# Latent attention scores in an fp32 encoder layer: six full matmuls per query tile, or four and a pair in row groups

## The chip, the cores and the metric

The kernel runs on one core of one Trainium2 chip. The core has a matrix engine (TensorE, PE in the profile), with its weight loads shown apart as PEld, and VectorE (DVE), ScalarE (ACT), GpSimd (POOL) and SyncE (SP). SP only issues transfers here. The metric is the time of one execution in device microseconds; before the change it is 1594.84 us, the median of two runs (1594.51 and 1595.16).

## The reference

One encoder layer is applied to two token sequences (256 and 1024 tokens, width 1024). A combined input projection feeds two attention groups: multi-head latent attention with 8 heads (MLA) and 2-D neighbourhood attention with 8 heads (NA). The outputs are normalised, projected, added to the input, and a SwiGLU feed-forward layer follows. The change touches the scores of the latent attention alone:

```python
q = (rmsnorm(c_q, q_norm_g) @ w_uq).reshape(B, S, MLA_HEADS, MLA_QK_DIM)
kv = (rmsnorm(c_kv, kv_norm_g) @ w_ukv).reshape(...)
k_nope, v = kv[..., :MLA_NOPE_DIM], kv[..., MLA_NOPE_DIM:]
q = concatenate([q[..., :64], apply_rope(q[..., 64:], cos, sin)], -1) * 96 ** -0.5
k_rope = apply_rope(k_r, cos, sin)           # one for all heads
s = einsum(qi[..., :64], k_nope) + einsum(qi[..., 64:], k_rope)
p = softmax(s)
o = einsum(p, v)
```

So a score sums over 96 features: 64 that each head has for itself ("nope") and 32 rotary ones, whose keys all heads share.

## The kernel before, in words

All large products are made from numbers split in two, a high part `h` and a rest `l`, both in the type fp32r. A product is then hh + hl + lh: three matmuls that accumulate in one PSUM bank (`mm3`, lines 109 to 113). The scores use it too: with 96 rows in use of the 128 (64 nope rows, 32 rotary rows, 32 rows set to zero by `zero_spare`), a query tile of 128 queries against 1024 keys takes two halves of 512 keys with three matmuls each, six in all.

The stages follow one another: latents and rotary parts, NA projections, NA itself, MLA (the stage of the change), output projection, feed-forward. MLA goes over four pairs of heads (`PAIRS`, index `p`). In a pair, `attend` handles blocks of 256 queries: `c` counts four such blocks of the long sequence ("sample"), `i` the two heads of the pair. So there are 4 x 4 x 2 = 32 sample blocks with two query tiles `u` each, and 8 blocks of the short sequence ("prompt"). For a query tile, TensorE makes the scores `S` (1024 keys, two PSUM banks; two such tiles exist, `S0` and `S1`), DVE takes the row maximum `mm`, ACT the exponential `ex` with its sum, TensorE transposes `ex` in eight pieces into `tp`, and ACT and DVE split them into `PT`. TensorE then multiplies `PT` with the values (`o`, 16 matmuls for a block) and transposes the result back twice (`os`, `ob`); POOL adds the halves, scales (`at`), and ACT's queue stores to `a_d`. Between blocks, the projections of the next pair's queries and keys run (`project_pair`, `project_rest`, tiles `SH`), which borrow the banks of `S0` for that time.

Queries lie in tiles `mq` (slots A, B, C in turn), keys in `mk` (slots e, o). Their rotary rows are read from DRAM (`rope_d`, `kr_d`), put there by an earlier stage; their nope rows are split out of PSUM by `put_q` and `split_k`.

A scheduler orders the instructions of every engine but one. SP's are left in the order of the program text (`manual_schedule` with SP), so a load that waits there for its tile to come free holds back all loads behind it. Transfers by `load_r` go on SP's queue, those by `store_r` on ACT's.

Of the kernel before, what the change touches and what calls it, by code (L numbers as in the profile page):

```python
# [19 lines left out]
P = 128  # L20
# [9 lines left out]
DH = 64  # L30
# [10 lines left out]
def encoder_trunk(ctx: ExitStack, tc: tile.TileContext, x_tm, x_T, g_attn, w_c, w_v, w_qk,  # L41
# [544 lines left out]
    def small_w(src, n):  # L586
        raw = lw.tile([P, 512], F32, name="w2_raw", bufs=2)
# [5 lines left out]

    cT = [[None] * 5 for _ in range(2)]
# [9 lines left out]
    def make_V():  # L604
# [9 lines left out]
        for i in range(2):  # L614
            for x in (q_slot[1][i], q_slot[2][i]):
                zero_spare(x, i)
# [6 lines left out]

    def q_tile(p, i, ch):
        x = qp_slot[i] if ch == 0 else q_slot[(2 * p + ch - 1) % 3][i]
        r0, hrow = 64 - 32 * i, 32 * ((2 * p + i) % 4)
        a, n = CHUNKS[ch]
        load_r(x[r0:r0 + 32],
               rope_d[p // 2, :, hrow:hrow + 32, a:a + n].rearrange("s p t -> p s t"))
        return x  # L630

    def k_tile(p, i, ch):
# [3 lines left out]
        if p < 2 and (ch == 1 or p == 0):  # L636
# [4 lines left out]
    def put_q(x, i, ps):  # L641
        rs = slice(64 * i, 64 * i + 64)
        split_ps_scaled(x[rs, 0], x[rs, 1], ps[rs], QSCALE)
# [13 lines left out]
    def split_k(K, ch, o, n, ps):  # L657
# [3 lines left out]
        for i in range(2):  # L661
            rs = slice(64 * i, 64 * i + 64)
            nc.vector.tensor_sub(out=K[i][ch][rs, 1, o:o + n], in0=ps[rs],
                                 in1=K[i][ch][rs, 0, o:o + n])

    def project_first():
# [3 lines left out]
        wq = small_w(w_qn[0], 3)  # L670
        K = [[k_tile(0, i, ch) for ch in range(2)] for i in range(2)]
        for s in range(2):
            load_cT(0, 3, s)
        for c in range(2):
            raw = lw.tile([P, 512], F32, name="w2_raw", bufs=2)
# [5 lines left out]
        for i in range(2):  # L681
            for x in (q_slot[0][i], qp_slot[i]):
                zero_spare(x, i)
# [3 lines left out]
        def body(bank):  # L687
# [13 lines left out]
            for i in range(2):  # L701
                put_q(Q[i][0], i, ps[:, 256:512])
# [10 lines left out]
    def project_pair(p):  # L713
# [5 lines left out]
        def body(bank):  # L719
# [7 lines left out]
            for i in range(2):  # L727
                put_q(Q[i][0], i, ps)
# [15 lines left out]
    def attend(p, Q, K, c_lo, c_hi, sample, between=None):  # L744
# [6 lines left out]
        for c in range(c_lo, c_hi):  # L751
            for i in range(2):
# [8 lines left out]
                else:  # L761
                    both = rp.tile([P, 2, 2, 256], F32R, name="PT", bufs=6)
                    pt = [[both[:, 0]], [both[:, 1]]]
                for u in range(2):
# [30 lines left out]
                for u in range(2):  # L795
# [6 lines left out]
                nc.gpsimd.tensor_tensor(out=ob[:, :, 0], in0=ob[:, :, 0], in1=ob[:, :, 1],  # L802
                                        op=ALU.add)
                if i == 0:
                    at = p2.tile([P, 2, P], F32, name="at", bufs=2)
                nc.gpsimd.tensor_tensor(out=at[:, :, i * DH:(i + 1) * DH], in0=ob[:, :, 0],
# [977 lines left out]
```

## Time and profile before

| | |
|---|---|
| median of the runs | 1594.84 us |
| the profiled execution's own time | 1593.86 us |
| its span | 1591.8 us |
| PE busy | 1559.4 us (98%), 8560 matmuls |
| PEld busy | 1394.9 us (88%) |
| DVE, ACT, POOL busy | 1016.4, 760.2, 766.4 us |
| MLA, about 380 to 672 us of the span: share of the span | 18% |

Busy time on PE is the union of its records. A record runs from the start of a matmul to its modelled end, so records of matmuls that follow one another overlap; how much time a matmul takes from TensorE is read from the distance of starts, not from its duration. The trace names a line of a helper where a helper issues the instruction: `L111`, `L112` and `L113` are the three matmuls of `mm3`, whoever calls it.

### The profile page before, as it was taken

The page shows a single profiled execution, that of the slowest core. Times are in us where ns is not written, and L with a number is a line of the kernel's source. Part 1 is how long each engine was busy: PE and PEld are TensorE (multiplying, and loading weights), DVE is VectorE, ACT ScalarE, POOL GpSimd, SP SyncE. Part 2 cuts the span into 40 slices and gives each one's busy share as a digit, 9 for nine tenths or more (in the row PEclk, how much of TensorE's full clock was granted, in tenths as well). Part 3 has the DMA queues.
Part 4 walks back from the last instruction along what each step waited for, and adds up shares of the span by engine and source line. Part 5 has one row for each costly group of instructions (what it writes and reads, how often), then busy time and mean ns, then how long its engine had stood idle before and what let it go on. Part 6 is the DMA issues. An engine that isn't in the chain of part 4 may idle for free.

```text
span 1591.8 us, 23991 instructions
## 1 busy us (share of the span) xinstructions
PE 1559.4 (98%) x8560; PEld 1394.9 (88%) x8560; DVE 1016.4 (64%) x1656; ACT 760.2 (48%) x1552; POOL 766.4 (48%) x961
## 2 busy tenths in 40 slices
PE   8999999999999999999999999999999999999998
PEld 8888789998888888877799999999999988888886
DVE  5754035556777777535698766566766666886676
ACT  6534144455777777633344344444334353443334
POOL 4632235544211119359626888788888871010002
PEclk9999999999999999999999999999999999999999
DMA  8626022243101021285573232223322237843434
GB/s 288 206 73 167 17 54 64 38 169 107 32 15 30 20 97 38 69 274 202 193 247 110 85 103 78 100 88 111 111 77 98 83 131 286 292 120 99 151 104 157
DMA packets 118022, 190.38 MB, mean 120 GB/s; under 512 B 34960, under 2 KB 65424, under 8 KB 115344
## 3 DMA queue, kind: packets, MB, share of 16 engines
q1 hardware_dynamic: 85216, 162.64, 31.4%
q10 hardware_dynamic: 31872, 23.14, 4.6%
q0 software_dynamic: 816, 3.08, 0.5%
q8 instruction: 67, 1.10, 0.3%
q14 instruction: 51, 0.42, 0.1%
HBM read 128.92 MB, written 59.90 MB: 119 GB/s over the span
## 4 chain that ended last, share of the span: by engine, by line
PE 83%; POOL 6%; DMA 3%; DVE 3%; ACT 3%; issue 2%; SPq 0%; POOLq 0%; ACTq 0%; DVEq 0%
PE M L113 10%; PE M L111 10%; PE M L112 10%; PE d L111 6%; PE d L113 6%; PE d L112 6%; PE o L789 4%; PE tp L779 3%; PE na_o L513 3%; PE pj L111 2%; PE pj L112 2%; PE pj L113 2%; PE S L111 2%; PE S L113 2%; PE S L112 2%
## 5 line engine op out<-in xcount | busy, mean ns | idle before, releaser
L1242 DVE TENSOR_TENSOR C<-M,C 128x428 f32<-128x428 f32 (+1 forms) x263 | 151.0, 594 | 144.0 <-issue 68.1
L1023 POOL TENSOR_TENSOR wr<-wt,wr 128x512 fp32r<-128x512 f32 (+1 forms) x106 | 148.9, 1405 | 67.4 <-ACT wr L1021 67.3
L1021 ACT CAST wr<-wt 128x512 fp32r<-128x512 f32 (+1 forms) x106 | 63.2, 599 | 134.2 <-PE M L112 123.7
L111 PE MATMUL M<-s,wr 128*128 128x428 f32 x352 | 125.9, 358 | 1.2 <-ACT x L970 1.2
L112 PE MATMUL M<-s,wr 128*128 128x428 f32 x352 | 125.4, 356 | 0.0
L113 PE MATMUL M<-s,wr 128*128 128x428 f32 x352 | 125.3, 357 | 0.0
L101 DVE TENSOR_TENSOR PT<-tp,PT 128x512 fp32r<-128x512 f32 (+1 forms) x144 | 93.4, 658 | 35.4 <-ACT PT L100 34.2
L1244 ACT COPY C<-M 128x428 f32<-128x428 f32 (+1 forms) x128 | 63.3, 514 | 84.6 <-PE M L113 84.6
L111 PE MATMUL M<-x,wr 128*128 128x428 f32 x264 | 94.2, 357 | 1.5 <-DVE C L1242 1.4
L100 ACT CAST PT<-tp 128x512 fp32r<-128x512 f32 (+1 forms) x144 | 79.4, 568 | 33.4 <-PE tp L779 30.2
L802 POOL TENSOR_TENSOR ob<-ob 128x128 f32<-128x128 f32 x40 | 18.4, 461 | 158.5 <-ACT ob L799 155.1
L771 DVE TENSOR_REDUCE mm<-S 128x1 f32<-128x1024 f32 (+1 forms) x80 | 85.0, 1062 | 13.8 <-PE S L113 12.3
L113 PE MATMUL M<-x,wr 128*128 128x428 f32 x264 | 91.5, 357 | 0.5 <-POOL wr L1023 0.3
L112 PE MATMUL d<-SE 128*128 128x512 f32 (+1 forms) x238 | 91.7, 387 | 0.0
L111 PE MATMUL d<-SE 128*128 128x512 f32 (+1 forms) x238 | 89.6, 388 | 0.0
L113 PE MATMUL d<-SE 128*128 128x512 f32 (+1 forms) x238 | 89.6, 387 | 0.0
L1284 ACT CAST SE<-as 128x640 fp32r<-128x640 f32 x58 | 42.2, 727 | 94.8 <-issue 57.2
L773 ACT ACTIVATE ex<-S,mm 128x1024 f32<-128x1024 f32 (+1 forms) x80 | 79.8, 998 | 14.9 <-DVE mm L771 13.6
L779 PE MATMUL tp<-ident,ex 128*128 128x128 f32 x544 | 79.2, 274 | 2.4 <-DVE PT L101 1.3
L789 PE MATMUL o<-PT,v 128*128 128x256 f32 x544 | 80.6, 287 | 0.8 <-ACT PT L100 0.8
L90 POOL TENSOR_SCALAR ry<-ssy 128x1 f32<-128x1 f32 x5 | 4.1, 820 | 157.6 <-ACT yo L1574 157.5
L111 PE MATMUL M<-SE,wr 128*128 128x428 f32 x220 | 78.6, 357 | 0.3 <-ACT C L1244 0.3
(466 smaller groups left out, 4909.1 us busy)
## 6 DMA issues: line engine op xcount, KB each, us to landing
as<-act_d SPq DMA_DIRECT2D x73, 320.0 KB
act_d<-C SPq DMA_DIRECT2D x70, 320.0 KB
w<-in_w_down_dram SPq DMA_DIRECT2D x44, 256.0 KB
x<-in_x_tm_dram SPq DMA_DIRECT2D x20, 512.0 KB
wr<-wop_d SPq DMA_DIRECT2D x20, 512.0 KB
wraw<-in_w_gate_dram SPq DMA_DIRECT2D x10, 1024.0 KB
wraw<-in_w_up_dram SPq DMA_DIRECT2D x10, 1024.0 KB
wop_d<-wr SPq DMA_DIRECT2D x18, 512.0 KB
```

The costliest lines, as they stand in the source:

```text
L100: i = nc.scalar.copy(out=hi, in_=ps)
L101: nc.vector.tensor_sub(out=lo, in0=ps, in1=hi)
L111: nc.tensor.matmul(out, lhsT=sh, rhs=mh, start=first, stop=False, **kw)
L112: nc.tensor.matmul(out, lhsT=sh, rhs=ml, start=False, stop=False, **kw)
L113: return nc.tensor.matmul(out, lhsT=sl, rhs=mh, start=False, stop=last, **kw).ins
L771: nc.vector.reduce_max(out=nm[:, u:u + 1], in_=S, axis=AX.X, negate=True)
L773: nc.scalar.activation(ex, S, AF.Exp, bias=nm[:, u:u + 1], scale=1.0, accum_out=l[:, u:u + 1])
L779: nc.tensor.transpose(tp[:, j], ex[:, kt * P:(kt + 1) * P], ident)
L789: nc.tensor.matmul(oT, lhsT=vv, rhs=pt[s][g][:, j], start=kt == 0 and s == 0, stop=kt == nkt - 1 and s == 1)
L1023: i1 = (eng or nc.gpsimd).tensor_tensor(out=lo, in0=raw_, in1=hi, op=SUB)
L1242: evicted[0] = nc.vector.tensor_add(out=o, in0=ps[:, 0:XN[j]], in1=o).ins
L1244: nc.scalar.copy(out=o, in_=ps[:, 0:XN[j]])
```

## The change

For the sample blocks the 288 rows of a score (three products of 96) are laid out anew. A query tile and a key tile have two planes of 128 rows each. For one head of a pair, with its own 64 rows first:

| rows | plane 0, query x key | plane 1, query x key |
|---|---|---|
| own 64 | q_h x k_h (nope) | q_l x k_h (nope) |
| other 64 | rotary: q_h x k_l and q_l x k_h, 32 rows each | q_h x k_l (nope) |

What is left is the rotary q_h x k_h, 32 rows. It is made by matmuls of 32 rows from two new tiles: `k_rot` holds the rotary keys' high part four times, in partitions 0, 32, 64, 96 (keys 0 to 511 and 512 to 1023, twice), and `rot` the rotary queries of one block, once for each of these. A query tile so takes four matmuls of 128 rows and two of 32 rows, which lie in two different row groups of the array (groups 0 and 1 for `u` = 0, groups 2 and 3 for `u` = 1). Prompt blocks keep `mm3`.

With it: `put_q` copies the high query part a second time, on ACT; `split_k` writes the rest of the keys into the other half and copies the high part once more, on POOL; the rows set to zero go for sample tiles; `rot_tile` issues four small loads per block, on SP, or on ACT's queue for `c` of 1 to 3 in the last pair; `w2_raw` has one buffer and no longer two; in the last pair's `c` of 2 and 3 the two operations on `ob` and `at` run on DVE and no longer on POOL.

```diff
+    k_rot = rslot["p2"].tile([P, 512], F32R, name="k_rot")
...
+    def halves_of(i):
+        return slice(64 * i, 64 * i + 64), slice(64 - 64 * i, 128 - 64 * i)
...
+    def rot_tile(p, i, c):
+        x = p2.tile([P, P], F32R, name="rot", bufs=3)
+        hrow, a = 32 * ((2 * p + i) % 4), NTOK_P + 256 * c
+        for u in range(2):
+            for g in range(2):
+                o = 64 * u + 32 * g
+                (store_r if p == PAIRS - 1 and c else load_r)(
+                    x[o:o + 32], rope_d[p // 2, 0, hrow:hrow + 32, a + P * u:a + P * (u + 1)])
+        return x
...
+    def put_q(x, i, ps, sample=True):
+        own, oth = halves_of(i)
+        split_ps_scaled(x[own, 0], x[own, 1], ps[own], QSCALE)
+        if sample:
+            nc.scalar.activation(x[oth, 1], ps[own], AF.Copy, scale=QSCALE)
...
         for i in range(2):
-            rs = slice(64 * i, 64 * i + 64)
-            nc.vector.tensor_sub(out=K[i][ch][rs, 1, o:o + n], in0=ps[rs],
-                                 in1=K[i][ch][rs, 0, o:o + n])
+            own, oth = halves_of(i)
+            nc.vector.tensor_sub(out=K[i][ch][oth if ch else own, 1, o:o + n], in0=ps[own],
+                                 in1=K[i][ch][own, 0, o:o + n])
+            if ch:
+                nc.gpsimd.tensor_copy(out=K[i][ch][own, 1, o:o + n], in_=K[i][ch][own, 0, o:o + n])
...
+                if sample:
+                    rot = rot_tile(p, i, c)
+                    Ss = [s_tile() for _ in range(2)]
+                    for u in range(2):
+                        qs = slice(q0 + u * P, q0 + (u + 1) * P)
+                        for a in range(0, ntok, step):
+                            for s in range(2):
+                                full = nc.tensor.matmul(Ss[u][:, a:a + step], lhsT=q[:, s, qs],
+                                                        rhs=k[:, s, a:a + step], start=s == 0,
+                                                        stop=False).ins
+                    with ExitStack() as es:
+                        if p == 1 and c == 3:
+                            es.enter_context(tc.issue_after(full))
+                        for g in range(4):
+                            rows, a = slice(32 * g, 32 * g + 32), 512 * (g % 2)
+                            nc.tensor.matmul(Ss[g // 2][:, a:a + step], lhsT=rot[rows],
+                                             rhs=k_rot[rows], start=False, stop=True)
...
-                    S = s_tile()[:, 0:ntok]
-                    for a in range(0, ntok, step):
-                        mm3(S[:, a:a + step], q[:, 0, qs], q[:, 1, qs],
-                            k[:, 0, a:a + step], k[:, 1, a:a + step], True, True)
+                    if sample:
+                        S = Ss[u]
+                    else:
+                        S = s_tile()[:, 0:ntok]
+                        mm3(S, q[:, 0, qs], q[:, 1, qs], k[:, 0], k[:, 1], True, True)
...
+                eng = nc.vector if p == PAIRS - 1 and c >= 2 else nc.gpsimd
```

The text issues the four matmuls of 32 rows together. TensorE's order shows where the scheduler puts them. Before, in the first pair of heads with queries of slot B (the last block of head 0), a query tile's six matmuls stand between transposes (`tp`) and transposes; S is the score tile, `mk0e` the keys, `mq0B` the queries:

```order
L779 MATMUL tp<-ident,ex 128x128 x4
L111 MATMUL S_5467<-mk0e,mq0B 128x512
L112 MATMUL S_5467<-mk0e,mq0B 128x512
L113 MATMUL S_5467<-mk0e,mq0B 128x512
L111 MATMUL S_5467<-mk0e,mq0B 128x512
L112 MATMUL S_5467<-mk0e,mq0B 128x512
L113 MATMUL S_5467<-mk0e,mq0B 128x512
L797 MATMUL o<-ident,os 128x128 x2
L779 MATMUL tp<-ident,ex 128x128 x8
```

Now, at the same place, with the next tile's scores behind it:

```order
L825 MATMUL tp<-ident,ex 128x128 x4
L799 MATMUL S_5484<-mk0e,mq0B 128x512 x4
L807 MATMUL S_5484<-k_rot,rot 128x512 x2
L843 MATMUL o<-ident,os 128x128 x2
L825 MATMUL tp<-ident,ex 128x128 x8
L799 MATMUL S_5571<-mk1e,mq1B 128x512 x4
L807 MATMUL S_5571<-k_rot,rot 128x512 x2
```

The six have become four and two: the matmuls of 32 rows stand in twos, those of one query tile, with full matmuls or transposes before and behind them, and not in fours.

On SP's queue, at the end of MLA's loads, before (`mq0A` to `mq1B` are the last pair's queries, `wo` the weights of the output projection):

```order
L77 DMA mq0A<-rope_d 32x2x512
L77 DMA mqp_4468<-rope_d 32x2x256
L77 DMA mq1A<-rope_d 32x2x512
L77 DMA mq0B<-rope_d 32x2x512
L77 DMA mq1B<-rope_d 32x2x512
L65 DMA gm<-in_g_mix_dram 128x8
L65 DMA wo_8144<-in_w_o_dram 128x1024 x2
```

and now:

```order
L77 DMA mq0A<-rope_d 32x512 x2
L77 DMA mqp_4468<-rope_d 32x2x256
L77 DMA mq1A<-rope_d 32x512 x2
L77 DMA rot<-rope_d 32x128 x8
L77 DMA mq0B<-rope_d 32x512 x2
L77 DMA mq1B<-rope_d 32x512 x2
L77 DMA rot<-rope_d 32x128 x24
L65 DMA gm<-in_g_mix_dram 128x8
L65 DMA wo_8333<-in_w_o_dram 128x1024 x2
```

The first loads of `wo` stand behind 24 loads of `rot`, for six blocks; with three buffers, the last of these can be issued when the block three before it has made its scores.

More of the change, by code (lines that the diff above doesn't have):

```diff
@@ L586, in small_w @@
     def small_w(src, n):
-        raw = lw.tile([P, 512], F32, name="w2_raw", bufs=2)
+        raw = lw.tile([P, 512], F32, name="w2_raw")
         rv_ = raw[:, 0:n * P].rearrange("p (a b) -> p a b", b=P)
@@ L613, in make_V @@
             vt[t] = v
-        for i in range(2):
-            for x in (q_slot[1][i], q_slot[2][i]):
-                zero_spare(x, i)
     def zero_spare(x, i):
@@ L627, in q_tile @@
         a, n = CHUNKS[ch]
-        load_r(x[r0:r0 + 32],
-               rope_d[p // 2, :, hrow:hrow + 32, a:a + n].rearrange("s p t -> p s t"))
+        rot = rope_d[p // 2, :, hrow:hrow + 32, a:a + n]
+        if ch:
+            for s in range(2):
+                o = halves_of(i)[1].start + 32 * s
+                load_r(x[o:o + 32, 0], rot[s])
+        else:
+            load_r(x[r0:r0 + 32], rot.rearrange("s p t -> p s t"))
+        return x
[7 more added lines that the diff above has]
+                    x[o:o + 32], rope_d[p // 2, 0, hrow:hrow + 32, a + P * u:a + P * (u + 1)])
         return x
@@ L635, in k_tile @@
         a, n = ((0, 256), (256, 1024))[ch]
-        if p < 2 and (ch == 1 or p == 0):
+        if ch == 1 and p < 2:
+            for s in range(2):
+                o = halves_of(i)[1].start + 32 - 32 * s
+                load_r(x[o:o + 32, 0], kr_d[s, :, a:a + n])
+        elif p == 0:
             load_r(x[r0:r0 + 32], kr_d[:, :, a:a + n].rearrange("s p t -> p s t"))
@@ L674, in project_first @@
         for c in range(2):
-            raw = lw.tile([P, 512], F32, name="w2_raw", bufs=2)
+            raw = lw.tile([P, 512], F32, name="w2_raw")
             load(raw, w_uv[c])
@@ L681, in project_first @@
         for i in range(2):
-            for x in (q_slot[0][i], qp_slot[i]):
-                zero_spare(x, i)
+            zero_spare(qp_slot[i], i)
         def held(n):
@@ L763, in attend @@
                     pt = [[both[:, 0]], [both[:, 1]]]
+                if sample:
[4 more added lines that the diff above has]
+                        for a in range(0, ntok, step):
+                            for s in range(2):
+                                full = nc.tensor.matmul(Ss[u][:, a:a + step], lhsT=q[:, s, qs],
[4 more added lines that the diff above has]
+                            es.enter_context(tc.issue_after(full))
+                        for g in range(4):
+                            rows, a = slice(32 * g, 32 * g + 32), 512 * (g % 2)
+                            nc.tensor.matmul(Ss[g // 2][:, a:a + step], lhsT=rot[rows],
+                                             rhs=k_rot[rows], start=False, stop=True)
                 for u in range(2):
```

19 lines of the change are left out of this document (9 added, 10 removed).

## The prediction

> **What bounds the kernel now.** I read the page first, then TensorE step by step in the stage of the change, then who it waits for there.
>
> On the page, the busy shares, the granted clock in 40 slices and the chain that ended last:
>
> ```profile
> span 1591.8 us, 23991 instructions
> PE 1559.4 (98%) x8560; PEld 1394.9 (88%) x8560; DVE 1016.4 (64%) x1656; ACT 760.2 (48%) x1552; POOL 766.4 (48%) x961
> ...
> PEclk9999999999999999999999999999999999999999
> ...
> PE 83%; POOL 6%; DMA 3%; DVE 3%; ACT 3%; issue 2%; SPq 0%; POOLq 0%; ACTq 0%; DVEq 0%
> ```
>
> TensorE is the bound, at its full clock. The stage of the change is as full: the same view by stretches (us, then busy time and count of PE, PEld, DVE, ACT, POOL, then clock and DMA) shows two periods of a head pair and the last pair with its end.
>
> ```profile
> 499.00:568.00 69.00, 67.92 (x448) 59.85 (x447) 51.44 (x79) 51.23 (x109) 11.16 (x24) 1.00 0.09 25
> 568.00:662.00 94.00, 92.42 (x626) 81.86 (x625) 69.33 (x103) 72.49 (x156) 52.08 (x60) 1.00 0.23 74
> ```
>
> PE is busy 98% there too, ACT 74% and 77%, DVE 75% and 74%. And of the waits in this stage, all that PE had are these (us in total, times, longest):
>
> ```profile
> PE tp L779 <- DVE PT L101: 1.3, 3, 0.7
> PE tp L779 <- ACT ex L773: 0.9, 3, 0.3
> PE o L789 <- ACT PT L100: 0.8, 4, 0.2
> PE S L111 <- ACT ex L773: 0.7, 3, 0.2
> ```
>
> 3.7 us in some 290: what TensorE is spared here comes off the end, and what it is given is added, until another engine is late.
>
> **A step of TensorE.** Busy time doesn't price a matmul, since records overlap. The timeline of PE does, by the distance of starts:
>
> ```profile
> 442.30 0.39 PE L112 MATMUL S<-mk1e,mq1B 128*128 128x512 f32 x1
> ...
> 444.86 0.38 PE L797 MATMUL o<-ident,os 128*128 128x128 f32 x2
> ...
> 452.11 1.04 PE L779 MATMUL tp<-ident,ex 128*128 128x128 f32 x8
> 452.90 0.48 PE L111 MATMUL S<-mk1e,mq1B 128*128 128x512 f32 x1
> 453.21 0.39 PE L112 MATMUL S<-mk1e,mq1B 128*128 128x512 f32 x1
> ```
>
> Between 442.30 and 444.86 eleven score matmuls start: 2.56 / 11 = 0.233 us for a full step, though a record lasts 0.39. From 452.11 to 453.21 are eight transposes and one full step: (1.10 - 0.233) / 8 = 0.108 for a transpose. Its 128 moving columns are a quarter of 512, but it takes more than a quarter of 0.233, 0.058. The weight loads, one per matmul, are at hand:
>
> ```profile
> 441.12 0.86 PEld L779 LDWEIGHTS tp<-ident,ex 128*128 128x128 f32 x8 [0.17 <-ACT ex L773]
> ...
> 442.30 0.19 PEld L113 LDWEIGHTS S<-mk1e,mq1B 128*128 128x128 f32 x1
> 442.53 0.19 PEld L111 LDWEIGHTS S<-mk1e,mq1B 128*128 128x128 f32 x1
> ```
>
> A load lasts 0.19 and begins when the matmul before its own starts (442.30, 442.53): one load ahead, hidden behind a full step, but in a row of transposes the loads set the pace, about 0.1 us apart.
>
> **What is removed and added on TensorE.** The count of query tiles:
>
> ```profile
> L771 DVE TENSOR_REDUCE mm<-S x80: 412/1224/1227, 382.2 to 654.2; 128x1 f32<-128x1024 f32 x64, 128x1 f32<-128x256 f32 x16
> ```
>
> 64 tiles have 1024 keys. Each had six full steps and gets four and a pair of 32 rows; two steps, 0.466 us, stand against the pair. All 64 together are 29.8 us. The order shows that the pair is alone, so it is two matmuls that can run together, not four. No matmul of before uses a part of the rows' groups in that way, so the pair's price is bounded. Both together, as one step: 0.233. One after the other: 0.466. Between: both stream together, but the second starts when its own load is in. If that is a load's distance behind the first, 0.108, the pair takes 0.341; if a whole load, 0.19, it takes 0.423. I take 0.341: loads go ahead of a matmul by one in the rows above, and the pair wants two. Saved: 64 x (0.466 - 0.341) = 8.0 us, with 64 x 0.233 = 14.9 and 64 x 0.043 = 2.8 as ends. Two blocks (second pair of heads, `c` = 3) have their four together, worth at most 1 us more; left out.
>
> The Trainium skill, TensorE: Matmul & The Clock Gate, section Part 3: Packing small matmuls, gives a speedup of 3.07 for four such row tiles with 512 columns. By it four take 1.30 steps; if a pair took as much, an estimate, 0.303, the saving would be 10.4 us. No run here shows it yet.
>
> **What else changes, and what hides it.**
>
> ```profile
> L105 ACT ACTIVATE mq1C<-SH 64x512 fp32r<-64x512 f32 x2 | 1.2, 596 | 0.0
> L68 ACTq DMA_DIRECT2D a_d<-at x20: 366/367/377, 418.9 to 672.5; - x20
> L486 POOL CAST qz<-qb 64x128 fp32r<-64x128 f32 x13 | 3.8, 293 | 11.4 <-PE na_s L488 11.1
> L622 POOL MEMSET mk0e<- 32x512 f32 x4 | 1.9, 520 | 0.1
> L802 POOL TENSOR_TENSOR ob<-ob 128x128 f32<-128x128 f32 x40 | 18.4, 461 | 158.5 <-ACT ob L799 155.1 <-DVE mr L801 3.4
> ```
>
> ACT gets 16 second copies of queries (four pairs, two heads, two chunks) at 0.596 = 9.5 us, and in the last pair 24 issues of `rot` at 0.367 = 8.8 us, each ahead of exponentials and splits for which TensorE waits. In a middle period ACT goes from 51.2 of 69 to about 53.6 of 67 (80%), in the last stretch from 72.5 of 94 to about 83.7 of 92 (91%). It stays under PE, but PE's waits for ACT, 2.4 us (0.9 + 0.8 + 0.7), grow: I take +1.5, between 0 (all in ACT's gaps) and 8.8 (each issue in full on the path).
>
> POOL gets 16 copies of keys, 64x512. By the nearest rows one lasts 0.5 (a memset of 512 columns) to 1.2 us (four of the 64x128 copies). Twelve fall where POOL sits idle (158.5 us before `ob` alone). The first four fall into NA, ahead of the `qz` copies that NA's matmuls need, 2 to 4.8 us; but eight memsets of `mk` at 0.52, 4.2 us, go from the same queue there. I take 0, between -2 and +1. The eight `ob` and `at` operations that go to DVE are about 3.5 us in the last stretch, where DVE has 24.7 us idle: 0.
>
> SP gets 104 issues of `rot`, which also go ahead of the next pair's weights and of `wo`. SP, POOL and PE at that place:
>
> ```profile
> 567.74 0.30 SPq L77 DMA_DIRECT2D mq1B<-rope_d  x1
> ...
> 568.56 18.77 SPq L65 DMA_DIRECT2D wo<-in_w_o_dram  x6
> ```
> ```profile
> 588.10 0.48 PE L111 MATMUL S<-mk0e,mq0C 128*128 128x512 f32 x1
> ...
> 661.81 0.50 PE L111 MATMUL po<-wo,mT 128*128 128x512 f32 x1
> ```
> ```profile
> 598.01 1.13 POOL L863 TENSOR_SCALAR wo<-wo,gm 128x1024 f32<-128x1024 f32 x1
> ...
> 636.72 2.39 POOL L97 TENSOR_TENSOR wo<-mT,wo 128x1024 fp32r<-128x1024 f32 x1
> ```
>
> `wo` was issued from 568.56. Now its loads wait until the third pair's last block of head 0 has made its scores, 589 on this clock, some 20 us later. POOL begins on `wo` at 598.0, so its start has 9 us left for the first load, and its end at 639.1 lies 22.7 us ahead of the first use at 661.8. Cost 0 behind that cover; beyond it PE waits one for one. The next pairs' weights wait in the same way for a block four blocks ahead of their use, about 25 us: 0, as long as `w2_raw` with one buffer (a split of 1.5 us between two loads) is all that is added.
>
> **Sum.** -8.0 + 1.5 = -6.5. The profiled execution took 1593.86 (its span 1591.8 and 2.06 around it): 1587.4. It lies 0.98 under the median of the runs, 1594.84, which is less than the terms are uncertain by; I say 1587.
>
> **Rivals.**
>
> *The array empties between kinds.* A record of a full matmul lasts 0.39 against a step of 0.233: 0.16 us pass between its last column and its end. If a change between 128 rows and 32 rows lets no matmul in until the one before has ended, each pair pays this twice, 0.32. The pair, at best 0.233, then costs 0.553, and 64 x (0.553 - 0.466) = +5.6, with ACT's 1.5: 1601, slower than before. With the pair at 0.341 it is +12.5 + 1.5: 1608. It decides against the change from 0.116 us per switch on (half of 0.233). Against it: the change from transposes to full matmuls costs nothing in the rows above; but both use all rows. The Trainium skill, TensorEngine Tiling (Array Packing), section Key Properties, states that changing the tiling mode drains TensorE. Chance 0.25.
>
> *The pair doesn't run together.* Then the change doesn't do what it says: 0.466 for 0.466, and only ACT's 1.5 remains: 1595. For it: each of the two waits for a load of its own rows, and no row shows two matmuls at once. Chance 0.13.
>
> *TensorE's gain is given back.* ACT's 24 issues in the last pair all end up ahead of a late exponential (+8.8 for 1.5), or `wo` is late: -8.0 + 8.8, 1595, up to 1602. For it: ACT at 91% in the last stretch. Against: its idle time there, 21.5 us, is over twice the 8.8. Chance 0.07.
>
> **How the numbers follow.** The forecast, that pairs overlap wholly or in part and no switch is paid, has 0.55 and goes from 1593.86 - 14.9 + 1.5 = 1580 to 1593.86 - 2.8 + 1.5 = 1593. The range 1579 to 1602 adds the two cases at 1595 and the half of the first rival with the better pair; what is left out is its worse half and a gain in NA's order, under 0.2. Over 2%, about what a measurement of this kernel tells from no change, is 32 us. Faster by that would take more than the whole second step of every tile (14.9) and all of PE's waits: 0.01. Slower by that needs 0.5 us for each tile more than the two steps taken away, a pair of 0.97; both rivals' prices at once give 0.79: 0.02. Within 2%: 0.97.
>
> **What would show it.** In the timeline of PE, the distance from the first of the 32-row matmuls to what comes behind the second: 0.341 by my step, 0.23 if both go at once, 0.47 if not. The start of the first one after the last full matmul, and of the next transposes after the pair, should be 0.233 and no later; 0.16 more at either is the first rival. PE's waits on ACT should stay under 4 us in the stage, `po` should not wait for `wo`, and the stretch of 69 us of a pair of heads should last 67. I am wrong if that stretch lasts as long as before or longer.

## The result and the profile after

The changed kernel takes 1617.62 us (median of 1617.30 and 1617.93) where the kernel before takes 1594.84: 22.8 us more, a ratio of 1.0143 with a 95% interval of 1.0099 to 1.0186. The prediction was 1587 us, in a range of 1579 to 1602. It had the sign wrong, and the result lies beyond its range.

The page of the changed kernel, whose profiled execution took 1617.93 us:

```profile
span 1616.2 us, 24171 instructions
...
PE 1571.1 (97%) x8560; PEld 1379.1 (85%) x8560; DVE 1018.8 (63%) x1664; ACT 769.1 (48%) x1568; POOL 758.7 (47%) x941
...
PEclk9999999999999999999999999999999999999999
...
PE 82%; POOL 6%; ACT 3%; DVE 3%; issue 3%; DMA 3%; SPq 1%; ACTq 0%; POOLq 0%; DVEq 0%
```

TensorE is the bound as before, at full clock but for one stretch of 3.4 us that is looked at below. It is busy 11.7 us longer, and the span has grown by 24.4. So about one half is work that got dearer, and the other is time in which TensorE stood still.

All of it lies in the latent stage. NA's last matmul starts 380.5 us into the span in both kernels; the last transpose of the stage starts at 662.7 before and at 687.8 after; from there to the end the two agree within 0.9 us. I cut the stage where TensorE starts the prompt block of each head pair. That gives a start, three periods in which the next pair's projections are made, and an end that has no projections:

| | start | period 1 | period 2 | period 3 | end | sum |
|---|---|---|---|---|---|---|
| before | 22.4 | 70.0 | 68.8 | 68.9 | 52.2 | 282.2 |
| after | 22.6 | 76.1 | 76.6 | 77.9 | 54.1 | 307.4 |

The view by stretches shows the third period and the end, of before and then of after (us from:to, length, then busy time and count of PE, PEld, DVE, ACT, POOL, then clock and DMA):

```profile
541.60:610.50 68.90, 67.81 (x447) 59.72 (x446) 51.32 (x79) 51.12 (x109) 20.06 (x29) 1.00 0.25 81
610.50:662.70 52.20, 50.83 (x350) 44.88 (x349) 37.94 (x60) 42.04 (x94) 36.75 (x44) 1.00 0.14 44
```
```profile
555.80:633.70 77.90, 72.58 (x447) 56.83 (x446) 51.86 (x79) 53.17 (x113) 24.01 (x34) 0.98 0.25 80
633.70:687.80 54.10, 52.47 (x350) 41.61 (x349) 38.24 (x64) 42.11 (x94) 32.80 (x39) 1.00 0.17 48
```

The end has 12 query tiles and lost 1.9 us, 0.16 a tile. It still is 97% busy, so there the work itself is dearer. The third period has 16 tiles and lost 9.0, of which PE's busy time is 4.8; the other 4.2 are idle time. ACT is no busier than 53.2 of 77.9 there. The clock of 0.98 in that period is one stretch behind a wait (after, same columns):

```profile
598.20:601.60 3.40, 3.40 (x12) 2.66 (x12) 0.86 (x2) 2.31 (x5) 0.86 (x2) 0.50 0.13 39
```

At half the clock for 3.4 us TensorE loses up to 1.7 us, which counts as busy time. The kernel before has no such stretch in this stage; some of the kernels below have up to four, and their sums hold that loss.

**Why a tile is dearer.** The timeline of PE in the changed kernel:

```profile
447.16 1.19 PE L799 MATMUL S<-mk1e,mq1B 128*128 128x512 f32 x4
448.28 0.50 PE L807 MATMUL S<-k_rot,rot 32*128 32x512 f32 x2
448.70 1.20 PE L799 MATMUL S<-mk1e,mq1B 128*128 128x512 f32 x4
449.83 0.50 PE L807 MATMUL S<-k_rot,rot 32*128 32x512 f32 x2
450.26 1.18 PE L825 MATMUL tp<-ident,ex 128*128 128x128 f32 x8
```

The two 32-row matmuls do run together: one's record lasts 0.495 in the mean, and both fit into 0.50 (the median distance of their starts in the trace is 0.003 us). But from the pair's start to the next matmul are 0.43 us (448.28 to 448.70, 449.83 to 450.26), not 0.341. And the four full matmuls between two pairs, 448.70 to 449.83, take 1.13, where four steps are 0.93: 0.2 are lost at their two ends. This tile takes 1.56 (448.70 to 450.26), where six full steps were 1.40. I call such a stay of TensorE in 32-row matmuls, from the last full matmul before it to the first behind it, a visit.

The weight loads show what happens at the border (same kernel, same place):

```profile
448.27 0.18 PEld L807 LDWEIGHTS S<-k_rot,rot 32*128 32x128 f32 x2 [0.37 <-issue]
448.70 0.76 PEld L799 LDWEIGHTS S<-mk1e,mq1B 128*128 128x128 f32 x4 [0.24 <-ACT PT L100]
449.83 0.18 PEld L807 LDWEIGHTS S<-k_rot,rot 32*128 32x128 f32 x2 [0.36 <-issue]
```

The loads of the 32-row weights aren't made ahead, during the last full step, but together with the pair, after 0.36 to 0.37 of idle time; and the next full load starts with its matmul too. At such a border no load runs ahead.

**Where TensorE stands still.** Its waits in the stage, 4.8 us in all before and 16.7 now, the five largest:

```profile
PE tp L825 <- ACT ex L819: 4.1, 5, 1.1
PE o L835 <- ACT PT L100: 4.1, 7, 0.9
PE S L799 <- ACT ex L819: 3.6, 8, 0.7
PE tp L825 <- DVE PT L101: 1.6, 4, 0.7
PE o L843 <- ACT os L839: 1.4, 3, 0.5
```

Most stand beside the projections, where the banks of `S0` are lent. The timeline there, of before, from the first query copy to the first scores that use the bank again:

```profile
501.86 0.59 ACT L105 ACTIVATE mq0C<-SH 64x512 fp32r<-64x512 f32 x1 [0.39 <-PE SH L649]
502.49 0.68 DVE L106 SCALAR_TENSOR_TENSOR mq0C<-SH,mq0C 64x512 fp32r<-64x512 f32 x1 [0.54 <-ACT mq0C L105]
...
503.67 0.59 ACT L105 ACTIVATE mq1C<-SH 64x512 fp32r<-64x512 f32 x1
...
504.30 0.69 DVE L106 SCALAR_TENSOR_TENSOR mq1C<-SH,mq1C 64x512 fp32r<-64x512 f32 x1 [1.13 <-ACT mq1C L105]
...
505.48 0.48 PE L111 MATMUL S<-mk0o,mq0A 128*128 128x512 f32 x1
```

And of after, with the second copy in line 667:

```profile
512.27 0.59 ACT L105 ACTIVATE mq0C<-SH 64x512 fp32r<-64x512 f32 x1 [1.27 <-PE SH L673]
512.89 0.68 DVE L106 SCALAR_TENSOR_TENSOR mq0C<-SH,mq0C 64x512 fp32r<-64x512 f32 x1 [1.06 <-ACT mq0C L105]
...
513.61 0.59 ACT L667 ACTIVATE mq0C<-SH 64x512 fp32r<-64x512 f32 x1 [0.75 <-DVE mq0C L106]
514.21 0.59 ACT L105 ACTIVATE mq1C<-SH 64x512 fp32r<-64x512 f32 x1
...
516.20 0.60 ACT L667 ACTIVATE mq1C<-SH 64x512 fp32r<-64x512 f32 x1
...
517.28 1.09 PE L799 MATMUL S<-mk0o,mq0A 128*128 128x512 f32 x4
```

The bank is read three times, in series: ACT, DVE, ACT. ACT stands still for 0.75 us until DVE is done, and the bank is free 4.5 us after the first copy began (516.80 - 512.27), not 3.1 (504.99 - 501.86).

### The profile page after: what moved, and what is told of

It reads as the page before. It is cut to its first block, busy times and chain, and to the rows that moved or that the text cites. A ratio compares the mean times of both kernels' runs of the same rounds, so it can differ in the third digit from the quotient of the medians.

```text
span 1616.2 us, 24171 instructions
## 1 busy us (share of the span) xinstructions
PE 1571.1 (97%) x8560; PEld 1379.1 (85%) x8560; DVE 1018.8 (63%) x1664; ACT 769.1 (48%) x1568; POOL 758.7 (47%) x941
## 4 chain that ended last, share of the span: by engine, by line
PE 82%; POOL 6%; ACT 3%; DVE 3%; issue 3%; DMA 3%; SPq 1%; ACTq 0%; POOLq 0%; DVEq 0%
PE M L111 10%; PE M L113 10%; PE M L112 10%; PE d L111 5%; PE d L113 5%; PE d L112 5%; PE o L835 4%; PE S L799 3%; PE tp L825 3%; PE na_o L513 3%; PE pj L111 2%; PE pj L112 2%; PE pj L113 2%; PE SH L673 2%; PE S L807 1%
## 5 line engine op out<-in xcount | busy, mean ns | idle before, releaser
L100 ACT CAST PT<-tp 128x512 fp32r<-128x512 f32 (+1 forms) x144 | 79.1, 567 | 33.2 <-PE tp L825 28.1
L835 PEld LDWEIGHTS o<-PT,v 128*128 128x128 f32 x544 | 69.9, 188 | 13.5 <-ACT PT L100 6.7
```

The source lines that it names most:

```text
L100: i = nc.scalar.copy(out=hi, in_=ps)
L835: nc.tensor.matmul(oT, lhsT=vv, rhs=pt[s][g][:, j], start=kt == 0 and s == 0, stop=kt == nkt - 1 and s == 1)
```

## The experiments

Theories at the start: **P**, the pair costs more than the two steps it replaces, because of what is lost where full matmuls and 32-row matmuls meet (the prediction's first rival); **W**, the waits beside the projections come from the second query copy by ACT, which holds the lent bank longer. Each was first tried by taking it out of the changed kernel, then by putting it alone into the kernel before. The first eight runs are one execution each, with one of the kernel before beside them (1594.35 for the first four, 1595.12 for the next four), so a difference of 2 us or less in their totals says little (all executions of the kernel before lie between 1592.31 and 1596.51); the others have four executions or more, with seven or more of the kernel before.

### The pair

Full rows: the pair takes all 128 rows of its tiles, and so adds products of other rows to the scores.

```diff
-                            rows, a = slice(32 * g, 32 * g + 32), 512 * (g % 2)
+                            rows, a = slice(0, P), 512 * (g % 2)
```

> The changed kernel, but each of the two rotary matmuls takes all 128 rows of its two tiles in place of 32, so no matmul uses a part of the rows (it adds products of other rows, so the scores are not the reference's; TensorE's order stays the same). Theory P, the loss of the pair is paid at the change between 128 and 32 rows: in the trace of the changed kernel a pair costs 0.093 us at its start, 0.430 until the next start and 0.06 to 0.10 behind it, about 0.61, against 0.466 for two full steps; 64 x 0.145 = 9.3 us less, 1608. Rival W, all of the loss comes from TensorE's waits on ACT and DVE: no more than 2 us less, 1616 to 1618.

Measured: 1612.75, the end of the stage 52.2 as before, the three periods 73.5, 76.1, 75.9. The stage is 7.3 shorter (300.1), 0.11 a tile; 2 us of it were given back behind the stage. The border is gone:

```profile
446.20 0.62 PE L807 MATMUL S<-k_rot,rot 128*128 128x512 f32 x2
446.66 1.10 PE L799 MATMUL S<-mk1e,mq1B 128*128 128x512 f32 x4
```

Two full steps are 0.46, and the next full matmul comes right behind. So two matmuls of 128 rows, one after the other, are cheaper here than two of 32 rows at once.

Same group: both matmuls of a pair in one row group, so that they can't run together (half of the keys get a wrong rotary part).

```diff
-                            rows, a = slice(32 * g, 32 * g + 32), 512 * (g % 2)
+                            rows, a = slice(64 * (g // 2), 64 * (g // 2) + 32), 512 * (g % 2)
```

> The changed kernel, but both matmuls of a pair use the same row group (the second one multiplies the first one's 32 rows, so half of the keys get a wrong rotary part; nothing else is changed). Theory P, the two run at once because they lie in different groups: now one follows the other, 0.21 to 0.23 us more for each of 64 pairs, 1631 to 1633. Rival, they didn't run at once and the 0.43 us are two matmuls in a row: no change, 1617 to 1618.

Measured: 1627.32, 9.7 more than the change. From the pair's start to the next matmul are now 0.66:

```profile
448.81 0.73 PE L807 MATMUL S<-k_rot,rot 32*128 32x512 f32 x2
449.47 1.19 PE L799 MATMUL S<-mk1e,mq1B 128*128 128x512 f32 x4
```

So in different row groups the two do run at once; it spares 0.23 of a visit, and not enough. The total misses what was expected, 1631 to 1633: 64 times 0.23 would be 14.7, and the stage grew by 9.5. TensorE's waits in the stage are some 3 us shorter here than in the change (13.6 and 16.7), which is more than half of the rest.

The pair alone, in the kernel before: the last two of a tile's six full matmuls become a pair of 32-row matmuls on the same tiles (the product of the low query part with the high key part is cut to these 32 rows).

```diff
+                            nc.tensor.matmul(S[:, a:a + step], lhsT=q[:, 0, qs],
+                                             rhs=k[:, 0, a:a + step], start=True, stop=False)
+                            nc.tensor.matmul(S[:, a:a + step], lhsT=q[:, 0, qs],
+                                             rhs=k[:, 1, a:a + step], start=False, stop=False)
...
+                        for g in (2 * u, 2 * u + 1):
+                            rows, a = slice(32 * g, 32 * g + 32), 512 * (g % 2)
+                            nc.tensor.matmul(S[:, a:a + step], lhsT=q[rows, 1, qs],
+                                             rhs=k[rows, 0, a:a + step], start=False, stop=True)
```

> The kernel before, with nothing of the change but the pair: each sample tile takes four full matmuls, and in place of the last two a pair of 32-row matmuls from the tiles it has (the score lacks the l x h product and has others, so it is not the reference's; no copies, loads or waits are added, and TensorE's order stays that of before). Theory P, a pair costs about 0.61 us against 0.466 because TensorE pays at the change between 128 and 32 rows, on both sides: 64 x (0.12 to 0.16) = 8 to 10 us more than before, 1602 to 1605. Rival, what the prediction had, pairs without a price at the change: 8 us less, 1586. If 1594: the pair is even.

Measured: 1598.63, 3.5 above before; the stage is 5.8 longer (periods 71.4, 70.2, 70.2, end 53.3), 0.09 a tile. PE's waits stay as before, and ACT, DVE and POOL do the same work. Here the steps stand one by one:

```profile
429.84 0.40 PE L770 MATMUL S<-mk1e,mq1A 128*128 128x512 f32 x1
430.07 0.39 PE L772 MATMUL S<-mk1e,mq1A 128*128 128x512 f32 x1
430.40 0.50 PE L780 MATMUL S<-mk1e,mq1A 32*128 32x512 f32 x2
430.82 0.74 PE L800 MATMUL o<-PT,v 128*128 128x256 f32 x4
```

From full to full 0.23, from full to the pair 0.33, from the pair to the next 0.42. So the pair, without anything else of the change, makes this kernel slower. It is a smaller part of the 22.8 than P had said. Tile by tile, from the second full matmul to the third matmul behind the pair, both kernels' traces show the same price over six full steps: 0.11 us where transposes follow, 0.16 to 0.17 where products with the values do. Summed over the stage that is more than the 5.8 that the stage grew, so a part is taken back elsewhere.

### The second query copy

By POOL, out of SBUF, in the changed kernel:

```diff
-            nc.scalar.activation(x[oth, 1], ps[own], AF.Copy, scale=QSCALE)
+            nc.gpsimd.tensor_copy(out=x[oth, 1], in_=x[own, 0])
```

> The changed kernel, but the second copy of the queries' high part is made by POOL from the first copy in SBUF, and no longer by ACT from the projection's PSUM bank (same result). Theory W, the part of the loss that is not the pair's price (24.3 - 9.3 = 15 us) comes from this copy, which makes the borrowed banks of S0 come free later and holds ACT while it waits for DVE: 8 to 15 us less, 1603 to 1610. Rival, those waits come from the new order and the new loads and stay: 1615 to 1618.

Measured: 1605.49, 12.1 less than the change: the larger part of the loss.

That, and full rows for the pair:

> Both edits at once: queries copied by POOL, and the rotary matmuls with all 128 rows (scores not the reference's). If the pair's price (9.3) and the copy's place (8 to 15) are the whole loss: 1594 to 1600, within a few us of before. If something else holds (loads of rot, POOL's copies of the keys, the new layout): 1600 to 1608.

Measured: 1602.19, 7.8 above before, in the range of the second theory. Something is left when both are gone. The same with the scores made tile by tile, as the text of before has them, and the four together nowhere:

```diff
-                    Ss = [s_tile() for _ in range(2)]
-                    for u in range(2):
...
+                        S = s_tile()
+                        for a in range(0, ntok, step):
```

> As e4 (queries copied by POOL, rotary matmuls of 128 rows, scores not the reference's), and the scores of each query tile are made inside the loop over its own u, as before, without the hold that makes two blocks of the second pair of heads wait for all eight full matmuls. e4 is 7.8 us above before, with the same count of full steps. If the text's order and that hold make the rest: 1595 to 1599. If the loads of rot, POOL's copies or the tiles do: 1600 to 1603.

Measured: 1602.30. It isn't the form of the loop. And the other way, the four together in all blocks of `c` = 2 and 3:

```diff
-                        if p == 1 and c == 3:
+                        if c >= 2:
```

> As e3 (queries copied by POOL, same result), and the hold that makes the four 32-row matmuls wait for all eight full ones stands in all blocks of c 2 and 3, so that 16 blocks have their four together. Theory P: four together cost what two do, about 0.61, so each such block spares one price: up to 14 x 0.6 = 8.5 us less than e3's 1605.5, 1597, if TensorE doesn't wait for it. Rival: in the two blocks that have the hold now, a block takes 7.5 to 7.9 us, against 6.9 in the others, since both score tiles must come free before the softmax of either begins; then 14 x 0.8 = 11 us more, 1617.

Measured: 1612.19, worse than the version it was made from by 6.7, where a gain of up to 8.5 was thought possible and the rival had a loss of 11. PE's waits of scores on the exponential grew from 1.8 to 7.5 us:

```profile
PE S L799 <- ACT ex L819: 7.5, 14, 0.7
```

Four at once need both score tiles free at the same time. TensorE spares a border and loses the tile that it had in hand.

The second copy alone, in the kernel before (into a tile that nobody reads; one `w2_raw` buffer to make room for it):

```diff
+        if x.shape[-1] == 512:
+            nc.scalar.activation(q_more[64 - 64 * i:128 - 64 * i], ps[rs], AF.Copy, scale=QSCALE)
```

> The kernel before, with nothing of the change but the second copy of each sample query chunk by ACT out of the projection's bank (16 copies, into a tile that nobody reads) and one buffer for w2_raw: same result. Theory W, the copy delays the release of the borrowed banks and holds ACT behind DVE: 8 to 13 us more than before, 1602 to 1607. Rival, the copy is only that dear in the changed kernel's order, or fits in ACT's gaps here: 0 to 4 us, 1594 to 1598.

Measured: 1611.06, 15.9 above before, more than W had said. Its edit has three parts, which the next runs tell apart: the single buffer; the bank held longer; ACT's time.

```diff
-        raw = lw.tile([P, 512], F32, name="w2_raw", bufs=2)
+        raw = lw.tile([P, 512], F32, name="w2_raw")
```

> The kernel before with one buffer in place of two for the raw weights w2_raw of the latent stage (which the change also takes, to make room), and nothing else. The kernel before with the second query copy had this edit in it too, so a part of its +16 us could come from here. Theory N (the buffer costs nothing: the raw weights are needed once in some 35 us and the split by POOL is short): 1593 to 1597 us. Rival R (the loads of the next weights come late and the projections wait for them): 1599 to 1606 us, with waits of the projections' matmuls on POOL or on the loads.

```diff
+        if x.shape[-1] == 512:
+            nc.scalar.activation(ps[rs], ps[rs], AF.Copy, scale=QSCALE)
```

> The kernel before, with both buffers of w2_raw, plus one extra ACT pass per 512-wide query chunk and head over the same bank (it scales the bank in place once the hi and lo parts have been read, and nobody reads it after that; the result is the reference's). It holds the bank as the change's second query copy does, with no other edit. Theory W (the copy's hold on the lent bank is the larger part of the loss, by itself): 1603 to 1612 us, PE waits in the projection regions of 10 to 17 us in all where the kernel before has 4 to 5. If the +16 us seen with the copy into another tile came from the single w2_raw buffer: 1595 to 1600 us.

```diff
+        if x.shape[-1] == 512:
+            nc.scalar.copy(out=q_more[64 - 64 * i:128 - 64 * i], in_=x[rs, 0])
```

> The kernel before plus the same second ACT copy of every 512-wide query chunk into another tile, and the single w2_raw buffer, but the copy reads the hi part out of SBUF instead of the bank, so that the bank is free after DVE's pass as before. ACT's time is the same (some 16 copies). Theory W (the hold on the bank is what costs): 1594 to 1600 us, PE's waits as in the kernel before. Rival T (ACT's time at that place, 0.6 us for each copy ahead of the next exponentials, or the order that it brings on PE, is what costs): 1604 to 1612 us as with the copy out of the bank (1611.1).

Measured, with before at 1593.84: the single buffer 1595.20 (ratio 1.0009, 1.0000 to 1.0018), nearly nothing. The copy on the bank 1613.95 (1.0129, 1.0112 to 1.0146): 20 us, by itself. The copy out of SBUF 1603.93 (1.0065, 1.0050 to 1.0080): 10 us, with the single buffer's 1.4 in it. So neither theory has it all: half of the copy's price falls away with the hold on the bank, and half stays. The end of the stage, without projections, is 52.1 to 52.2 in all three. Of POOL's copies, put into the kernel before in the same manner (keys and queries, read by nobody):

```diff
+            nc.gpsimd.tensor_copy(out=more[64 - 64 * i:128 - 64 * i], in_=x[rs, 0])
...
+                nc.gpsimd.tensor_copy(out=more[rs], in_=K[i][ch][rs, 0, o:o + n])
```

> The kernel before plus the change's POOL copies of the sample keys and, on POOL too, the second copy of the sample queries (both out of SBUF into a tile that nobody reads), with one w2_raw buffer. The versions of the change with the query copy on POOL stay 7 us above before even where the pair takes whole rows. Theory K (the copies on POOL, or the order that they bring, are that rest): 1599 to 1603 us. Rival L (POOL's copies cost nothing by themselves, the rest comes from the rotary loads on the queues, or from matmuls that must wait for the copies): 1593 to 1597 us.

Measured: 1603.38 (1.0058, 1.0042 to 1.0075), with before at 1593.44. Copies that no one reads, on an engine that idles, cost 10 us, again with the single buffer in it. In all these kernels PE's waits are mostly of one kind. In the one with the copy on the bank:

```profile
PE tp L781 <- ACT ex L775: 13.0, 12, 2.3
PE o L791 <- ACT PT L100: 3.0, 9, 0.5
PE S L111 <- ACT ex L775: 2.0, 6, 0.6
```

TensorE does not wait for the copy. It waits for exponentials.

### The copy or the order

The build orders the instructions by its own estimate of when each is ready. With a copy in the text, TensorE's order is another one: beside a projection, a score tile stands behind the projection and the transposes, and no longer ahead of them. For the copy on the bank, 426 of the stage's 1840 matmuls stand at another place than before. Now theory **O**: this order is what costs. Theory **H**: the copy itself does. The next kernels tie the 1840 matmuls of the stage to a given order, by an edge from each to the one before; MLA_ORDER lists that order.

```diff
+    for a, b in zip(seq, seq[1:]):
+        tc.add_manual_dep(mms[b], mms[a].name,
+                          mybir.DependencyInfo(mybir.DependencyClass.NoSync,
+                                               mybir.DependencyReason.DATA), reason="order")
```

The copy on the bank, with the order of before:

> The kernel before with the extra ACT pass over each query bank (as in the run with the copy that holds the bank, 1613.95 us), but with the 1840 matmuls of the latent stage kept, by explicit edges, in the very order of the kernel before. Theory O (the order of the matmuls that the build chose because of the copy is what costs, not the copy): 1594 to 1599 us. Theory H (the copy costs by itself, through ACT's time and the bank held longer): 1606 to 1614 us; half and half would lie near 1603.

The kernel before, with the order of the copy and no copy:

> The kernel before without any copy, its 1840 latent-stage matmuls kept in the order that the build chose for the kernel with the bank-holding copy. Theory O: 1606 to 1614 us. Theory H: 1593 to 1598 us.

Measured, with before at 1593.97: 1609.69 (1.0099, 1.0084 to 1.0114) and 1613.66 (1.0123, 1.0106 to 1.0139). Each theory is right in its own run. With the old order the copy costs 15.7, and PE waits for just that copy; the first row is of that kernel. With the new order there are 19.7 to pay even if the copy isn't there; the second row is of that one.

```profile
PE S L143 <- ACT SH L677: 11.5, 6, 2.7
```
```profile
PE tp L811 <- ACT ex L805: 15.2, 12, 2.4
```

Order and copy together were 20.1 (1613.95). So in the new order the copy is free, and the order costs all of it. As I read the two orders, the build put the scores behind other work so that the late bank doesn't hold TensorE up, and that work then waits for exponentials that were started late. It is one loss that shows at one place or the other.

The same order, on the change itself: with the copy by POOL, and with the copy by ACT (pairs in each tile's own loop).

> The change with the second query copy on POOL, each tile's pair in the tile's own loop, and the latent stage's matmuls in the order of before (a pair stands where the tile's last two full matmuls stood). Its result is the reference's. Theory O: before plus the pair's price alone, 1596 to 1601 us. Theory H: 1603 to 1607 us, as the change with the POOL copy and its own order (1605.5).

> As the run beside it, but with the second query copy on ACT out of the bank, as the change has it. Theory O: 1597 to 1603 us. Theory H: 1610 to 1618 us, little below the change itself (1617.6).

Measured: 1609.76 (1.0098, 1.0083 to 1.0113) and 1624.46 (1.0192, 1.0177 to 1.0207). Both are above what O and H had said for them, but the periods say where:

| | start | period 1 | period 2 | period 3 | end |
|---|---|---|---|---|---|
| before | 22.4 | 70.0 | 68.8 | 68.9 | 52.2 |
| before, copy on the bank, order of before | 22.4 | 75.4 | 73.0 | 74.5 | 52.2 |
| change, POOL copy, order of before | 28.1 | 72.3 | 71.3 | 71.5 | 55.3 |
| change, ACT copy, order of before | 28.6 | 76.8 | 77.2 | 76.3 | 55.3 |

The start is 6 us longer in the two kernels of the change, but not in the kernel with the same forced order and no other edit than the copy; it is looked at below. The end is 1.2 longer than with the change's own order, as long as one new wait on DVE there (1.2). In the three periods the sums over before are 15.2 for the copy on the bank, 7.4 for the change without it and 22.6 for the change with it; the change in its own order has 22.9.

These sums hold more than the copy and the pair. Of the 15.2, 11.5 are the waits shown above, and up to 3.4 are two stretches of 3.4 us at half the clock (at 429.4 and 576.1). Of the 7.4, 2.6 are waits on DVE's split of the prompt keys, one in each period:

```profile
PE o L705 <- DVE mkp L719: 2.6, 3, 0.9
```

The other 4.8 are 0.10 for each of 48 tiles, near the 0.09 of the pair alone. Of the 22.6, 10.5 are six waits on ACT's second copy, and up to 6.8 are 13.7 us at half the clock, all behind such waits; that leaves 5.3, or 0.11 a tile. That 15.2 + 7.4 is 22.6 to the tenth is luck, since the clock's parts differ; the waits on the copy (11.5 and 10.5) and the price of a pair (0.10 and 0.11) are what agrees.

Last, the copies that hold no bank, with the order of before: POOL's unread copies, and ACT's copy out of SBUF.

> The kernel before plus POOL's copies of sample keys and queries into a tile that nobody reads, one w2_raw buffer, and the 1840 matmuls of the latent stage in the order of before. Theory O2 (those unread copies cost only through the order that the build made for them, +9.9 us): 1593 to 1598 us, and the three periods of a head pair at 70, 69 and 69 us as before. Rival (POOL's work itself slows the stage, for instance DVE beside it): 1601 to 1605 us.

> The kernel before plus ACT's second query copy out of SBUF (no longer hold on the bank), one w2_raw buffer, and the order of before. Theory O2 (16 copies of 0.6 us fit into ACT's gaps when the order is the old one): 1594 to 1599 us. Rival (ACT's time at that place is on the path): 1602 to 1606 us, as with its own order (1603.9).

Measured, before at 1593.44: 1600.52 (1.0038, 1.0026 to 1.0051) and 1602.76 (1.0054, 1.0039 to 1.0069). The totals lie between the two theories or with the rival, but the start is again longer, 29.0 and 26.7 and not 22.4. The periods decide. With POOL's copies they are 69.9, 68.8 and 68.8, those of before to 0.1:

```profile
410.60:480.60 70.00, 69.44 (x456) 61.42 (x454) 51.69 (x79) 50.60 (x108) 17.68 (x36) 1.00 0.08 22
480.60:549.30 68.70, 67.63 (x447) 59.67 (x446) 51.24 (x79) 51.03 (x109) 15.91 (x33) 1.00 0.09 25
```

With ACT's copy out of SBUF they are 71.9, 70.5 and 70.5, 5.2 over before. With the build's own order these two kernels lose 11.0 and 11.3 in start and periods together (a start shorter by 2 goes with a longer first period there, as with the single buffer alone). So POOL's copies cost the periods nothing by themselves, and what these lose in the build's own order is order; ACT's time costs 5.2; the other 10 of the 15.2 go with the hold on the bank, the half clock behind its waits included.

The long start goes with the single buffer. All four kernels that have it together with the order of before start late; the two with a forced order and both buffers have 22.4 and 22.3. SP's queue, with both buffers (the copy on the bank, order of before) and with one (POOL's copies, order of before), and TensorE in the latter:

```profile
351.02 3.71 SPq L97 DMA_DIRECT2D w_raw<-in_w_uv_dram  x2
355.36 0.40 SPq L109 DMA_DIRECT2D mq0A<-rope_d  x1
```
```profile
356.16 25.35 SPq L97 DMA_DIRECT2D w_raw<-in_w_uv_dram  x2
382.11 0.35 SPq L109 DMA_DIRECT2D mq0A<-rope_d  x1
```
```profile
386.01 0.76 PE L143 MATMUL S<-mk0e,mq0A 128*128 128x512 f32 x1 [4.03 <-DMA mq0A<-rope_d]
```

With one buffer the second load of raw weights waits for the first's split, the load of `mq0A` behind it comes 27 us later, and the first scores wait 4.0 us for it; from 384.4 the clock is at half for 6.8 us. The single buffer in the build's own order has the same late load (380.8), but there TensorE has other matmuls ahead of it and waits 0.6. No run has the order of before and one buffer with nothing else, so how much the copies add there stays open.

No version of these was faster than the kernel before. With the old order and no cost of a copy in the periods, what is left there is the price of the pair and the 2.6 us of waits.

## Why the prediction was wrong

**The pair at 0.341: wrong.** The prediction let the second matmul start one load's distance after the first and charged nothing at either end. The second starts at once, so that part was too dear. But a visit takes 0.43 from its start, its entry is 0.33 and not 0.233, and the matmul behind it is late as well. The 64 tiles gave nothing like -8.0: the pair costs 0.09 (alone in before), 0.11 (against full rows in the change) to 0.16 us (end of the stage) more than two full steps, +6 to +10 in the stage. The first rival, "the array empties between kinds", has the right place, the change between 128 and 32 rows: it gave +5.6 (a pair of 0.553) and +12.5 as its two sizes, and the measured lie between. Its mechanism is not shown to the letter. The pair starts 0.33 after a full matmul whose record lasts 0.39, and the matmul behind it at 0.42 to 0.43 while the pair's record lasts 0.50, so each starts 0.06 to 0.08 before the modelled end that the rival let it wait for. Whether a partial emptying costs the time or the weight load that isn't made ahead, no run separates. Its own clue, the 0.16 us between a full matmul's last column and its end, was in the rows that the prediction quoted; what spoke against it (transposes and full matmuls follow each other at no cost) compared two kinds that both use all rows. The Trainium skill, TensorEngine Tiling (Array Packing), section Key Properties, has the rule that a change of the tiling mode drains TensorE; the trace agrees in kind, with 0.1 at the entry and no weight load ahead on either side. The figure of 3.07 in the Trainium skill, TensorE: Matmul & The Clock Gate, section Part 3: Packing small matmuls, isn't reached in a visit between full matmuls: four together take 0.43 until the next matmul and their late entry, 0.1, which is at most 1.75 times as fast as four full steps (0.93 / 0.53), and two are no faster at all.

**ACT at +1.5, between 0 and 8.8: wrong, and the larger miss.** The count was right: 16 copies of 0.59. The 24 issues on ACT's queue cost nothing that shows, since the end of the stage lost only the pair's price. But the prediction weighed the copies by ACT's busy share of a period. What counts is where they stand: on a bank that TensorE needs back, in series behind DVE, at the one place of a period in which no second score tile is in hand. That is 15.2 us over three periods with the order held, 11.5 of it in six waits and up to 3.4 by the half clock behind them, against 7.1 us that the 12 copies there last. For POOL and SP the prediction asked which use of TensorE waits for their work and how much time there is until then; for ACT it did not ask. Its waits of before were short by one, too: its four rows have 3.7 us, and one of 1.1 on DVE's `v` is not among them. And what it calls two periods and the last pair is one stretch as long as a period and one with the rest of the third period and the end.

**POOL's copies of keys at 0: right as work, wrong as a change.** They last 0.61 us and cost the periods nothing in the old order. But the build counts them too, and in the trial with the keys' and queries' copies together its new order cost some 11 us in start and periods. The prediction took it for granted that the order around the change stays.

**SP, `wo`, DVE at 0: right.** TensorE waits for no `wo`, and the eight operations on `ob` and `at` took 0.28 us each on DVE, beside other work. The single `w2_raw` buffer, taken as free, measured +1.4 us in the build's own order and 0.2 in the stage; with the order of before it goes with a start that is 4 to 7 us longer.

**What would show it.** The signs named there were the right ones, and all but one came out against the forecast: 0.43 behind the pair, 0.33 ahead of it, waits on ACT of over 13 us, periods of 76 to 78. Only the one on `po` and `wo` held. The range reached 1602 because the first rival was taken with its smaller size and ACT's bound stopped at 8.8, worked out from the issues alone; with the copies' place priced as well, by the runs above, it would have had to reach 1618 (1593.9, +9 for the pair and +15 for the copies).

## What to carry to other kernels

Matmuls of few rows in separate row groups run at once, but here a visit of them among full-row matmuls cost its entry and exit too (0.53 us for a pair, where two full steps are 0.47); for a few at a time, count the visit and not the matmuls. An operation that is added to a buffer which the bound engine is waiting to get back costs by its place in that chain, however idle its engine is on average. And where a build orders the instructions, a copy that no one reads can cost ten microseconds through the order alone: hold the order fixed before calling an operation dear, and compare stage by stage, clock included, since the forced order moved other waits.

## What was unexpected of the hardware

The price of a visit is the same with two row groups and with four. In the changed kernel the four of two tiles together take as long as a pair:

```profile
531.86 0.50 PE L807 MATMUL S<-k_rot,rot 32*128 32x512 f32 x4
532.29 0.44 PE L843 MATMUL o<-ident,os 128*128 128x128 f32 x2
```

0.43 for four (0.44 the other time) and 0.43 for two, 0.66 for two in one group. And weight loads, which run one matmul ahead among full rows, don't run ahead across the border.

A wait of the bound engine can cost more than itself. In the profiles of these kernels every stretch of half clock in the latent stage (3.4 or 6.8 us, in eleven of the twenty) begins in a wait of TensorE of 1 us or more or within 5 us behind one; a full step takes 0.43 us in it and not 0.23. Not every such wait has one: the kernel with the order alone waits up to 2.4 us at a time and keeps its clock in the stage.
